# Seven small changes in one: decoding of picks on fewer columns, picks turned into one PSUM bank, low parts of U made by VectorE from the last query on, and reordered ends

## The chip, the cores and the metric

One core of a Trainium2 chip. The metric is the device time in microseconds (us) of one execution; lower is better. TensorE is PE in the rows (PEld is its weight load), VectorE DVE, ScalarE ACT, GpSimd POOL; SP is the queue that issues most transfers.

## What is computed

One encoder layer over 512 tokens of width 1024, in float32:

```
h = rms_norm(x);  P = h @ w_in                      # u_A, v_A, q, k, v
A = gelu(u_A) * (w_s . layer_norm(gelu(v_A)) + b)   # position mixing in chunks of 128
B = dilated windowed attention, 8 heads
x = x + concat(rms_norm(A), rms_norm(B)) @ w_out
xn = rms_norm(x)                                    # then PEER, per token:
  s1, i1 = top16(q1 . keys1);  s2, i2 = top16(q2 . keys2)        # per head, 128 keys each
  sc, ci = top16(s1[:, None] + s2[None, :])
  e = i1[ci // 16] * 128 + i2[ci % 16];  g = softmax(sc)
  x = x + sum over heads, picks of g * gelu(xn . U[e]) * V[e]     # 16384 experts
out = rms_norm(x)
```

## The kernel before

**Products in float32.** Both operands are split into a high part (ScalarE cast, `L80`, `L170`) and a low part (source minus high part: `L81`, `L181`); three products are accumulated.

**Stages, in order of time.** (1) Five projections in `proj` (`L252`), with norms, rotation (`rotate`) and head transposes between; at `L146` a root on ScalarE gives `xrs`, with which `rotate` reads the first projection's banks. The sums of squares under that root are made by `xsq` (`L151`). After the third projection `va` (`L373`) reads its banks through Gelu. (2) Attention (`L412` to `L447`) and the output projection. (3) Sixteen query products (`query`, `scores`), whose scores VectorE ranks (`top16`, `L618` to `L626`). (4) Routing: `decode` turns a pick's place in a list of 54 candidates into a row and a column, and looks both up by a one-hot of 16 by 16 per pick (`L681` to `L697`), for heads in groups of 3, 3 and 2 (`HG`); then `softmax`. VectorE does nearly all of it. (5) The banks: `turn` transposes a block's picks (`L824`), ScalarE copies them out (`L829`), and for every 8 tokens `hots` makes two one-hots on VectorE (`L855`, `L859`) whose 16 products (`L896`) give a dense matrix of gates, evacuated by ScalarE (`L876`) and stored to DRAM (`L884`). (6) The expert loop over 128 blocks e of 128 experts: acc of all three token blocks takes V's product (`vproduct`, `L1041`), while U's product (`product`, `L201`) runs 36 blocks ahead, and the gate is multiplied in (`L1026`). The fourth token block (128 tokens) is done by gathers of rows instead (`gather`, on GpSimd, VectorE). (7) Last sums, norm and output.

**What sets the order.** Each engine runs its queue in the order of the program. From stage 3's end to stage 6, products of U are strewn in by `ahead(n, limit)`: n matmuls of the running block (24 a block); a block's start also issues the load of the block two later and the high part of the block one later. Its low part is made by GpSimd in two halves inside `product` as long as `prog["pool"]` holds, and by VectorE in `los()` after that; `prog["pool"]` falls after `turn(0)`. `uraw`, `uhi` and `ulo` have two buffers each, so the load of block i+2 starts when high and low part of block i are made. The Gelu of a finished block (`flush`, `L768`) frees one of two PSUM banks `pu`.

**The end.** For the last two e the order is: (126, token blocks 0 and 1), (127, 0), (127, 1), (126, 2), (127, 2 in halves). Per block: sum and square (`final_sum`, `L1081`), gain (`L1092`), `root`, `finish` (`L1106`, `L1108`), store.

Of the kernel before, what the change touches and what calls it, by code (L numbers as in the profile page):

```python
# [20 lines left out]
NB = 4  # L21
# [19 lines left out]
UVB = 4  # L41
SLOW = 0.35
# [3 lines left out]
def peer_block(ctx: ExitStack, tc: tile.TileContext, A, out):  # L46
# [182 lines left out]
    warm(AF.Copy)  # L229
# [79 lines left out]
    def xsq(b):  # L309
        sq = tk.tile([128, 1024], F32, name="xs", bufs=4)  # L310
        sumsq(sq, xt[:, b, :], xss[:, b:b + 1])
# [60 lines left out]
    for b in range(NB):  # L372
        S.activation(va[:, b, :], ps[b], AF.Gelu_apprx_tanh, scale=xrs[:, b:b + 1], accum_out=lns[:, 0, b:b + 1])  # L373
# [274 lines left out]
    def decode(pool, lists, ci, outs):  # L648
# [3 lines left out]
        tl = lambda nm, dt: pool.tile(PK, dt, name=nm)  # L652

# [23 lines left out]
        wide = [128, n, TOPK, TOPK]  # L677
        ohs = []
        for r in (rw, cl):
            oh = pool.tile([128, nh, nb, TOPK, TOPK], BF16, name="oh", bufs=3 if pool is rt else 2)  # L680
            S.copy(oh.rearrange("p h b r c -> p (h b) r c"),  # L681
                   r.rearrange("p h b k -> p (h b) k")[:, :, :, None].to_broadcast(wide))
            ohs.append(oh)
        yield
        io = iota_b[:, None, None, 0:TOPK].to_broadcast(wide)
        o4 = [oh.rearrange("p h b r c -> p (h b) r c") for oh in ohs]
        for o in o4:
            V.tensor_tensor(o, o, io, op=ALU.is_equal)
        for p, o in enumerate(o4):
            V.tensor_tensor(o, o, fi.rearrange("p h b s k -> p (h b) s k")[:, :, p, None, :].to_broadcast(wide),  # L690
                            op=ALU.mult)
        yield
        for w in (8, 4, 2):
            for o in o4:
                V.tensor_tensor(o[:, :, :, 0:w], o[:, :, :, 0:w], o[:, :, :, w:2 * w], op=ALU.add)
        for oh, o in zip(ohs, outs):
            V.tensor_tensor(o, oh[:, :, :, :, 0], oh[:, :, :, :, 1], op=ALU.add)  # L697
# [15 lines left out]
    HG = (3, 3, 2)  # L713
    route = [rt.tile([128, DB, H, TOPK], F32, name=f"route{i}") for i in range(3)]
# [38 lines left out]
    def pick_head(h):  # L753
# [3 lines left out]
        for n in HG:  # L757
            if h == h0 + n - 1:
                steps.append(decode(rt, dense[1][:, h0:h0 + n], ci[:, h0:h0 + n], [r[:, h0:h0 + n] for r in by_head]))
# [42 lines left out]
    while steps:  # L802
        ahead(24, AHEAD)
        flush()
# [5 lines left out]
    for _ in range(4):  # L810
        ahead(36, AHEAD)
        flush()
# [5 lines left out]
    def turn(b):  # L818

        rows = []  # L820
        for nm, t, dt, scale in (("i2T", route[1], BF16, 1.0), ("i1T", route[0], BF16, 1.0),
                                 ("gT", route[2], F32, GSCALE)):
            ps = pr.tile([128, 512], F32, name="po" if nm == "i2T" else "tr")
            T.transpose(ps[:, :128], t[:, b].rearrange("p h k -> p (h k)"), ident)  # L824
            if nm == "i2T":

                idx = rt.tile([128, 16, 2, 8, 2], BF16, name="idxT", bufs=2)
            r = idx[:, :, len(rows), :, :] if dt is BF16 else rt.tile([128, 16, 8, 2], F32, name=nm)
            S.activation(r, ps[:, :128].rearrange("p (g t) -> p g t", t=8)[:, :, :, None].to_broadcast([128, 16, 8, 2]),  # L829
                         AF.Copy, scale=scale)  # L830
# [11 lines left out]
    prog["pool"] = False  # L842
# [4 lines left out]
    def hots(t8):  # L847
# [3 lines left out]
        idx, gw = tsc[b]  # L851
# [389 lines left out]
```

## Time and profile before

| | us |
|---|---|
| median of 3 runs (1487.87 to 1490.42) | 1488.34 |
| the profiled execution | 1490.96 |
| its span in the trace | 1489.2 |
| TensorE busy in it | 1453.4 (98%) |
| VectorE busy | 1159.6 (78%) |
| ScalarE busy | 641.3 (43%) |
| GpSimd busy | 283.6 (19%) |
| mean granted TensorE clock | 0.996 of full |

Busy TensorE is modelled: what its queue loses is seen in gaps between starts, and in stretches with a granted clock below 1. Where a row ends in [0.50 <-ACT ...], the engine sat idle 0.50 us before, and that released it.

### The profile page before, as it was taken

To read this page: it belongs to the slowest core of one execution; us is meant where nothing else is said; L and a number is where in the kernel's file an instruction comes from. 1 tells how busy PE (TensorE), PEld (TensorE's weight loads), DVE (VectorE), ACT (ScalarE), POOL (GpSimd) and SP (SyncE) were. 2 spreads that over 40 slices of the span, in tenths; PEclk is the share of its full clock that TensorE was granted. 3 is DMA by queue.
4 is the path that set the end of the run, shared out by engine and by line. 5 is a ranking of instruction groups with operands and counts; after the bars stand their busy time and mean duration, and the time that the engine had idled before them with its cause. 6 is when DMAs were issued, how large, how long until landed. Compare 5 with 4: busy or idle time off the path is not lost.

```text
span 1489.2 us, 21574 instructions
## 1 busy us (share of the span) xinstructions
PE 1453.4 (98%) x7945; PEld 1292.6 (87%) x7945; DVE 1159.6 (78%) x2415; ACT 641.3 (43%) x1088; POOL 283.6 (19%) x222
## 2 busy tenths in 40 slices
PE   8999999999899999999999999999999999999997
PEld 6878988888888899999999999999999999987785
DVE  4745554999899967779878787888787888877775
ACT  5455753344555544434333333333333333323334
POOL 0040002445500000012222222222222222211002
PEclk9999999999999999999999999999999999999999
DMA  6331032232366776469999999999999998988764
GB/s 217 106 99 57 22 114 104 86 91 96 110 230 256 261 291 214 135 228 378 355 351 329 315 338 321 327 334 336 347 326 333 331 328 308 348 286 299 250 212 160
DMA packets 128777, 358.52 MB, mean 241 GB/s; under 512 B 9120, under 2 KB 59808, under 8 KB 112288
## 3 DMA queue, kind: packets, MB, share of 16 engines
q1 hardware_dynamic: 103184, 197.75, 40.1%
q0 software_dynamic: 18432, 134.23, 23.6%
q10 hardware_dynamic: 7056, 25.18, 4.2%
q8 instruction: 62, 1.02, 0.3%
q14 instruction: 43, 0.35, 0.1%
HBM read 327.10 MB, written 30.02 MB: 240 GB/s over the span
## 4 chain that ended last, share of the span: by engine, by line
PE 78%; DVE 9%; DMA 5%; issue 3%; ACT 3%; POOL 1%; ACTq 0%; SPq 0%; DVEq 0%; POOLq 0%
PE pu L201 34%; PE acc L1041 30%; PE acc L252 6%; DMA vraw<-in_uv_dram 3%; DVE ohb L855 3%; DVE oha L859 2%; DVE ulo L181 1%; DMA uraw<-in_uT_dram 1%; PE tr L734 1%; PE pu L252 1%; PE tr L434 1%; POOL ulo L181 1%; PE acc L447 1%; DVE vlo L81 1%; DMA xt<-in_x_dram 1%
## 5 line engine op out<-in xcount | busy, mean ns | idle before, releaser
L201 PE MATMUL pu<-h2T,uhi 128*128 128x384 f32 (+2 forms) x2336 | 451.0, 342 | 3.2 <-ACT act L768 2.4
L201 PEld LDWEIGHTS pu<-h2T,uhi 128*128 128x128 f32 x2336 | 409.6, 189 | 19.4 <-ACT act L768 3.1
L987 POOL DMA_INDIRECT uv<-in_uv_dram,ei x128 | 170.6, 1333 | 830.1 <-DVE xlast L1002 318.0
L81 DVE TENSOR_TENSOR vlo<-vraw,vhi 128x1024 fp32r<-128x1024 f32 x128 | 156.8, 1225 | 154.9 <-ACT vhi L80 154.7
L80 ACT CAST vhi<-vraw 128x1024 fp32r<-128x1024 f32 x128 | 134.6, 1051 | 296.3 <-issue 188.6
L1041 PE MATMUL acc<-vhi,wahi 128*128 128x512 f32 x768 | 238.7, 391 | 1.9 <-ACT wahi L80 1.9
L1041 PE MATMUL acc<-vlo,wahi 128*128 128x512 f32 x768 | 238.2, 391 | 0.5
L1041 PE MATMUL acc<-vhi,walo 128*128 128x512 f32 x768 | 237.8, 391 | 0.0
L201 PE MATMUL pu<-h2T,ulo 128*128 128x384 f32 (+2 forms) x1168 | 234.1, 340 | 2.3 <-POOL ulo L181 2.3
L201 PEld LDWEIGHTS pu<-h2T,ulo 128*128 128x128 f32 x1168 | 203.7, 188 | 7.4 <-POOL ulo L181 2.9
L170 ACT CAST uhi<-uraw 128x1024 fp32r<-128x1024 f32 x144 | 150.7, 1047 | 61.1 <-DMA uraw<-in_uT_dram 47.6
L1041 PEld LDWEIGHTS acc<-vlo,wahi 128*128 128x128 f32 x768 | 143.8, 188 | 33.7 <-DVE vlo L81 2.4
L1041 PEld LDWEIGHTS acc<-vhi,walo 128*128 128x128 f32 x768 | 143.7, 188 | 31.5 <-DVE walo L81 0.9
L1002 DVE SCALAR_TENSOR_TENSOR xlast<-uv,dot,xlast 128x1024 f32<-128x1024 f32 x128 | 164.5, 1285 | 4.5
L1041 PEld LDWEIGHTS acc<-vhi,wahi 128*128 128x128 f32 x768 | 142.6, 188 | 26.9 <-ACT wahi L80 3.1
L768 ACT ACTIVATE act<-pu 128x384 f32<-128x384 f32 x128 | 62.9, 492 | 234.9 <-PE pu L201 234.5
L993 DVE SCALAR_TENSOR_TENSOR uv<-uv,h 128x1024 f32<-128x1024 f32 x128 | 153.7, 1219 | 6.7 <-DMA uv<-in_uv_dram,ei 6.7
L181 DVE TENSOR_TENSOR ulo<-uraw,uhi 128x1024 fp32r<-128x1024 f32 x116 | 141.5, 1220 | 22.1 <-ACT uhi L170 21.9
L181 POOL TENSOR_TENSOR ulo<-uraw,uhi 128x512 fp32r<-128x512 f32 x56 | 81.5, 1479 | 209.4 <-ACT uhi L170 203.7
L81 DVE TENSOR_TENSOR walo<-wa,wahi 128x384 fp32r<-128x384 f32 x128 | 70.7, 553 | 0.6 <-ACT wahi L80 0.6
L80 ACT CAST wahi<-wa 128x384 fp32r<-128x384 f32 x128 | 65.2, 509 | 13.0 <-DVE wa L1026 12.9
L1026 DVE TENSOR_TENSOR wa<-act,wt 128x384 f32<-128x384 f32 x128 | 70.5, 551 | 0.0
(258 smaller groups left out, 1475.4 us busy)
## 6 DMA issues: line engine op xcount, KB each, us to landing
uraw<-in_uT_dram SPq DMA_DIRECT2D x128, 512.0 KB, 5.9
vraw<-in_uv_dram SPq DMA_DIRECT2D x128, 512.0 KB, 5.3
wd<-wst ACTq DMA_DIRECT2D x48, 512.0 KB, 3.1
wt<-wd SPq DMA_DIRECT2D x32, 768.0 KB, 10.6
wraw<-in_w_in_dram SPq DMA_DIRECT2D x19, 512.0 KB, 3.6
uraw<-in_w_q_dram SPq DMA_DIRECT2D x16, 512.0 KB, 3.8
xT<-in_xT_dram SPq DMA_DIRECT2D x8, 256.0 KB, 3.9
xt<-in_x_dram SPq DMA_DIRECT2D x1, 2048.0 KB, 11.5
```

Of the source, the lines that this page charges most:

```text
L80: S.copy(hi, src)
L81: sub.tensor_tensor(lo, src, hi.bitcast(F32), op=ALU.subtract)
L170: S.copy(hi, raws[i])
L181: eng.tensor_tensor(lo[:, k, :], raws[i][:, k, :], hi[:, k, :].bitcast(F32), op=ALU.subtract)
L201: T.matmul(o, l[:, k, :], r[:, k, t0:n], start=(p == 0 and k == 0), stop=(p == 2 and k == KT - 1))
L252: T.matmul(out[b], l[:, b * 128:(b + 1) * 128], r[:, kk, :], start=(k == 0 and i == 0), stop=(k == KT - 1 and i == 2))
L768: S.activation(acts[e], o[:, :DT], AF.Gelu_apprx_tanh)
L987: G.indirect_dma_start(out=uvs[r].rearrange("p s d -> p (s d)"), out_offset=None, in_=A["uv"], in_offset=bass.IndirectOffsetOnAxis(ap=ei[: ...
L993: V.scalar_tensor_tensor(uv[:, 0, :], uv[:, 0, :], 1.0, h2, op0=ALU.mult, op1=ALU.mult, accum_out=d[:, 0:1])
L1002: V.scalar_tensor_tensor(xlast, uv[:, 1, :], d[:, 1:2], xlast, op0=ALU.mult, op1=ALU.add)
L1026: eng.tensor_tensor(wa.rearrange("p (c t) -> p c t", c=NWC), acts.pop(e).rearrange("p (c t) -> p c t", c=NWC), wts[e // WG][:, :, e % WG, ...
L1041: T.matmul(acc[b][n], l[:, c], r[:, n * 512:(n + 1) * 512], start=(e == 0 and i == 0), stop=(e == NK - 1 and i == 2))
```

## The change

It joins these edits (the line numbers of the new kernel are up to 60 higher):

1. Start: the first table that ScalarE loads holds Sqrt; two of the four sums of squares of `xsq` go to VectorE.
2. `warm(Gelu)` ahead of the last transposed head pair; `va` reads banks 1, 2, 3, then 0.
3. `decode`: the 16 sorted picks use only columns 0 to 7 for the picks 0 to 7 and all 16 for the rest, so the one-hot has 24 rows of 8 instead of 16 of 16; ScalarE's broadcast copies and VectorE's products are two each; the constant `iota_v` is made by GpSimd.
4. `prog["pool"] = False` already after the last query, with `los()` behind every `ahead`: VectorE makes the low parts of 11 blocks that GpSimd made.
5. `turn` writes three transposes into one bank; the gates' table has another layout.
6. `hots`: VectorE makes 7 of the 8 tokens' gate rows, ScalarE the eighth (`gated`, two small activations per 8 tokens).
7. One block of U is put ahead of the last stores (and one fewer after them).
8. The end: block 2's products of the last four e come last, half by half; blocks 0 and 1 are finished under them; the last two e's parts lie in the gather's buffers, and gathers are due one e earlier.

```diff
-    warm(AF.Copy)
+    warm(AF.Sqrt)
...
+        if b % 2:
+            V.scalar_tensor_tensor(sq, xt[:, b, :], 1.0, xt[:, b, :], op0=ALU.mult, op1=ALU.mult,
+                                   accum_out=xss[:, b:b + 1])
+        else:
+            sumsq(sq, xt[:, b, :], xss[:, b:b + 1])
...
+        if p == 3:
+            warm(AF.Gelu_apprx_tanh)
...
-    for b in range(NB):
+    for b in (1, 2, 3, 0):
         S.activation(va[:, b, :], ps[b], AF.Gelu_apprx_tanh, ...
...
+            oh = pool.tile([128, n, TOPK + K8, K8], BF16, name="oh", bufs=3 if pool is rt else 2)
+            S.copy(oh[:, :, 0:TOPK, :], flat.to_broadcast([128, n, TOPK, K8]))
+            S.copy(oh[:, :, TOPK:, :], flat[:, :, K8:, :].to_broadcast([128, n, K8, K8]))
...
+            V.tensor_tensor(o, o, iota_v[:, None, :, :].to_broadcast([128, n, TOPK + K8, K8]), op=ALU.is_equal)
+            V.tensor_tensor(o[:, :, TOPK:, :], o[:, :, TOPK:, :], f[:, :, :, K8:].to_broadcast(...), op=ALU.mult)
+            V.tensor_tensor(o[:, :, 0:TOPK, :], o[:, :, 0:TOPK, :], f[:, :, :, 0:K8].to_broadcast(...), op=ALU.mult)
...
+            V.tensor_tensor(o[:, :, K8:TOPK, :], o[:, :, K8:TOPK, :], o[:, :, TOPK:, :], op=ALU.add)
+        for w in (4, 2):
...
         else:
+            prog["pool"] = False
             ahead(12, AHEAD)
+            los()
...
     while steps:
         ahead(24, AHEAD)
+        los()
         flush()
         step()
...
+        ps = pr.tile([128, 512], F32, name=("tr", "po")[b % 2])
+        for j, t in enumerate((route[1], route[0], route[2])):
+            T.transpose(ps[:, j * 128:(j + 1) * 128], t[:, b].rearrange("p h k -> p (h k)"), ident)
...
-        wide = [128, 2, 8, NK // 2, 2]
+        wide = [128, 7, 2, NK // 2, 2]
...
+    def gated():
+        for a, c, gs, g in rest:
+            for s in range(2):
+                S.activation(a[:, 14 + s, :], c[:, 15, :], AF.Copy, scale=gs[:, g, s:s + 1])
+        rest.clear()
...
+    ahead(10 ** 6, AHEAD)
+    ahead(24, AHEAD + 5)
+    los()
     for j in range(per):
         store(j)
-    ahead(10 ** 6, AHEAD)
+    flush()
...
-    for _ in range(3):
+    for _ in range(2):
         ahead(24, AHEAD + 5)
...
+    lasts = range(NK - LASTV, NK)
+    for e in lasts:
+        vproduct(e, 2, (0,))
     for b in (0, 1):
+        sumsq(junk, xback[b], sums[b][:, 0, 0:1])
+        rs = inv_root(ex, sums[b][:, 0, 0:1], 1024)
+        for c in (slice(0, 512), slice(512, 1024)):
+            V.scalar_tensor_tensor(outs[b][:, c], xback[b][:, c], rs, fg[:, c], op0=ALU.mult, op1=ALU.mult)
+            Q.dma_start(out[b * 128:(b + 1) * 128, c], outs[b][:, c])
+        if b == 0:
+            final_sum(2, 0, 0, 512)
+    gain(2, 0, 512, V)
+    for e in lasts:
+        vproduct(e, 2, (1,))
...
+    V.tensor_scalar(xback[2][:, :512], outs[2][:, :512], rs, None, op0=ALU.mult)
+    S.activation(xback[2][:, 512:], outs[2][:, 512:], AF.Copy, scale=rs)
+    for q, c in ((Q, slice(0, 512)), (S, slice(512, 1024))):
+        q.dma_start(out[256:384, c], xback[2][:, c])
```

**The order on VectorE, second group of heads of the routing.** `cand` is the last list of candidates, `oh` the one-hot, `route` the looked-up keys. Before:

```order
L642 TENSOR_TENSOR cand<-s_2179 128x3x12
L642 TENSOR_TENSOR cand<-s_2179 128x3x8
L688 TENSOR_TENSOR oh<-oh,iota_b 128x2304 x2
L690 TENSOR_TENSOR oh<-oh,fi 128x2304 x2
L695 TENSOR_TENSOR oh<-oh 128x144x8 x2
L695 TENSOR_TENSOR oh<-oh 128x144x4 x2
L695 TENSOR_TENSOR oh<-oh 128x144x2 x2
L697 TENSOR_TENSOR route_2183<-oh 128x3x3x16
```

Now:

```order
L648 TENSOR_TENSOR cand<-s_2179 128x3x8
L182 TENSOR_TENSOR ulo<-uraw,uhi 128x1024 x2
L702 TENSOR_TENSOR oh<-oh,iota_v 128x1728 x2
L705 TENSOR_TENSOR oh<-oh,fi 128x9x64
L707 TENSOR_TENSOR oh<-oh,fi 128x9x128
L705 TENSOR_TENSOR oh<-oh,fi 128x9x64
L707 TENSOR_TENSOR oh<-oh,fi 128x9x128
L182 TENSOR_TENSOR ulo<-uraw,uhi 128x1024
L711 TENSOR_TENSOR oh<-oh 128x9x64 x2
L714 TENSOR_TENSOR oh<-oh 128x9x16x4 x2
L714 TENSOR_TENSOR oh<-oh 128x9x16x2 x2
L717 TENSOR_TENSOR route_2186<-oh 128x3x3x16
```

Low parts now stand between the steps of the decoding; one more stands ahead of the last query's ranking.

**The order on VectorE, third group of heads.** `fi` holds the picked lists, `gsum` the softmax's sums. Now (before, no `ulo` stood here):

```order
L688 CAST fi<-i_2180 128x192
L182 TENSOR_TENSOR ulo<-uraw,uhi 128x1024 x3
L728 TENSOR_REDUCE gsum<-route_2188 128x24
L729 RECIPROCAL gsum<-gsum 128x24
L730 TENSOR_TENSOR route_2188<-route_2188,gsum 128x8x3x16
L182 TENSOR_TENSOR ulo<-uraw,uhi 128x1024
L702 TENSOR_TENSOR oh<-oh,iota_v 128x1152 x2
L705 TENSOR_TENSOR oh<-oh,fi 128x6x64
L707 TENSOR_TENSOR oh<-oh,fi 128x6x128
```

Three low parts in a row, then a fourth; two more follow before the last additions.

**The order on ScalarE at the last stores.** `wst` is the evacuation of the last banks, `act` a Gelu. Before:

```order
L876 ACTIVATE wst<-acc 128x128x4 x2
L884 DMA wd<-wst 128x1024 x4
L170 CAST uhi<-uraw 128x1024
L768 ACTIVATE act<-pu 128x384
```

Now:

```order
L910 ACTIVATE wst<-acc 128x128x4 x2
L171 CAST uhi<-uraw 128x1024
L918 DMA wd<-wst 128x1024 x4
L789 ACTIVATE act<-pu 128x384
```

The cast that the next block waits for stands ahead of the four issues.

## Rows read from the trace of the kernel before

**Rows 1.** Stretches of the span: from:to in us, length, busy time of each engine (instructions), granted TensorE clock, DMA share, GB/s. A piece of the expert loop, then the banks.

```profile
900.00:1100.00 200.00, 200.00 (x1012) 182.07 (x1011) 165.93 (x235) 73.76 (x132) 47.06 (x35) 1.00 0.92 329
404.00:541.20 137.20, 131.29 (x1241) 121.11 (x1238) 134.56 (x118) 80.62 (x140) 0.00 (x0) 1.00 0.66 244
```

**Rows 2.** What TensorE waited for: us in total, times, longest.

```profile
PE acc L896 <- DVE oha L859: 3.9, 10, 0.7
PE pu L201 <- ACT act L768: 2.4, 1, 2.4
PE pu L201 <- POOL ulo L181: 2.3, 2, 2.0
PE tr L824 <- ACT idxT L829: 2.1, 3, 0.8
PE acc L252 <- ACT qraw L270: 2.1, 1, 2.1
PE po L824 <- DVE route L697: 1.5, 1, 1.5
PE acc L252 <- ACT va L373: 1.3, 1, 1.3
```

**Rows 3.** The start of the second projection: ScalarE's instructions in order of time (start, us, what, idle before); then, from the groups (us in total, mean ns | idle), VectorE's instruction of the kind that now makes a sum of squares.

```profile
28.43 1.05 ACT L151 ACTIVATE xs<-xt 128x1024 f32<-128x1024 f32 x1
29.59 1.28 ACT L146 ACT_TABLE_LOAD   x1
30.88 0.30 ACT L146 ACTIVATE xrs<-xss,eps 128x4 f32<-128x4 f32 x1
...
L1002 DVE SCALAR_TENSOR_TENSOR xlast<-uv,dot,xlast 128x1024 f32<-128x1024 f32 x128 | 164.5, 1285 | 4.5
```

**Rows 4.** A stretch as in Rows 1, right behind that wait.

```profile
32.30:35.60 3.30, 3.30 (x9) 2.60 (x10) 2.69 (x5) 2.54 (x4) 0.00 (x0) 0.60 0.00 0
```

**Rows 5.** VectorE in the routing, in order of time (xN: so many in the time given).

```profile
350.78 0.19 DVE L660 TENSOR_SCALAR mk<-cf 128x144 f16<-128x144 f16 x1
350.90 1.34 DVE L666 TENSOR_TENSOR at<-at,mk 128x144 f16<-128x144 f16 x1
...
365.06 2.63 DVE L688 TENSOR_TENSOR oh<-oh,iota_b 128x2304 bf16<-128x2304 bf16 x2
...
370.13 2.92 DVE L695 TENSOR_TENSOR oh<-oh 128x1152 bf16<-128x1152 bf16 x6
...
382.21 1.22 DVE L671 TENSOR_SCALAR rw<-ai 128x96 int32<-128x96 int32 x1
...
389.10 2.92 DVE L690 TENSOR_TENSOR oh<-oh,fi 128x1536 bf16<-128x1536 bf16 x2
391.94 5.32 DVE L695 TENSOR_TENSOR oh<-oh 128x768 bf16<-128x768 bf16 x6
397.18 0.56 DVE L697 TENSOR_TENSOR route<-oh 128x96 f32<-128x96 bf16 x2
```

**Rows 6.** GpSimd's low part at the time of the first slow instruction of Rows 5.

```profile
350.87 2.53 POOL L181 TENSOR_TENSOR ulo<-uraw,uhi 128x512 fp32r<-128x512 f32 x2 [2.19 <-ACT uhi L170]
```

**Rows 7.** VectorE in the banks: the first one-hot, then a low part and the starts after it.

```profile
401.17 1.22 DVE L855 TENSOR_TENSOR ohb<-iota_b,idxT 128x2048 bf16<-128x2048 bf16 x1
...
405.96 1.22 DVE L181 TENSOR_TENSOR ulo<-uraw,uhi 128x1024 fp32r<-128x1024 f32 x1
407.09 1.22 DVE L855 TENSOR_TENSOR ohb<-iota_b,idxT 128x2048 bf16<-128x2048 bf16 x1
408.35 1.22 DVE L859 TENSOR_TENSOR oha<-ohb,gw 128x2048 f16<-128x2048 bf16 x1
409.49 1.22 DVE L855 TENSOR_TENSOR ohb<-iota_b,idxT 128x2048 bf16<-128x2048 bf16 x1
```

**Rows 8.** From the tile of U's loads, stretch 345 to 404 us: time from issue to landing; and a cast of a high part on ScalarE there.

```profile
DMA to landing us min/median/max: 3.5/3.7/4.2
...
397.00 1.05 ACT L170 CAST uhi<-uraw 128x1024 fp32r<-128x1024 f32 x1 [5.05 <-DMA uraw<-in_uT_dram]
```

**Rows 9.** TensorE, in order of time: where it went on after the first transposed picks; of the 48 groups of bank products two that follow each other, and the last.

```profile
399.13 0.94 PE L201 MATMUL pu<-h2T,uhi 128*128 128x384 f32 x4
...
430.78 1.06 PE L896 MATMUL acc<-oha,ohb 128*128 128x128 f16 x16
...
433.49 1.07 PE L896 MATMUL acc<-oha,ohb 128*128 128x128 f16 x16
...
540.29 1.07 PE L896 MATMUL acc<-oha,ohb 128*128 128x128 f16 x16 [0.68 <-DVE oha L859]
```

**Rows 10.** ScalarE's smallest copy of the kind that `gated` adds; TensorE behind the last stores.

```profile
398.34 0.38 ACT L829 ACTIVATE idxT<-po 128x256 bf16<-128x256 f32 x1
...
546.11 3.04 PE L201 MATMUL pu<-h2T,uhi 128*128 128x384 f32 x16 [0.50 <-ACT uhi L170]
```

**Rows 11.** The end: TensorE's last piece in the chain that ended last (start and length in us, tile, line, instructions), then VectorE's first sum and last scaling of token block 2.

```profile
1413.43 62.23 PE acc L1041 x273
...
1480.58 0.69 DVE L1081 TENSOR_TENSOR fin<-acc,fin 128x512 f32<-128x512 f32 x1
...
1484.70 0.88 DVE L1108 TENSOR_SCALAR fin<-fin,sd 128x512 f32<-128x512 f32 x2
```

**Rows 12.** The page: U's loads, 512 KB each, median us from issue to landing over the whole kernel.

```profile
uraw<-in_uT_dram SPq DMA_DIRECT2D x128, 512.0 KB, 5.9
```

More of the change, by code (lines that the diff above doesn't have):

```diff
@@ L41 @@
 UVB = 4
+LASTV = 4
 SLOW = 0.35
@@ L364, in peer_block @@
     turning = heads_T("k", rot)
-    for _ in range(4):
+    for p in range(4):
+        if p == 3:
+            warm(AF.Gelu_apprx_tanh)
         next(turning)
         drain(gen, 2)
-    warm(AF.Gelu_apprx_tanh)
     drain(gen)
@@ L646, in candidates, with lookup_rows, decode @@
         return cand
-    def decode(pool, lists, ci, outs):
+    def lookup_rows(pool):
+        rows = pool.tile([128, 24, 8], BF16, name="iota_v")
+        for r0, r1, c0 in ((0, 16, 0), (16, 24, 8)):
+            G.tensor_copy(rows[:, r0:r1, :], iota[:, None, c0:c0 + 8].to_broadcast([128, r1 - r0, 8]))
+        return rows
+    def decode(pool, iota_v, lists, ci, outs):
         _, nh, nb, _ = PK = list(ci.shape)
@@ L867, in peer_block @@
     hot = [hots(0), hots(1)]
+    gated()
     ahead(24, AHEAD)
@@ L895, in peer_block @@
                     t = 4 * q + j
-                    T.matmul(pw[:, j, :], c[:, t, :], a[:, 8 * s + t, :], start=(s == 0), stop=(s == 1))
+                    T.matmul(pw[:, j, :], c[:, t, :], a[:, 2 * t + s, :], start=(s == 0), stop=(s == 1))
             t0 = (t8 % per) * 8 + 4 * q
@@ L946, in decoded @@
         def decoded(h):
-            return decode(gp, late[1][:, h:h + 4], gci[:, h:h + 4], [r[:, h:h + 4] for r in groute])
+            return decode(gp, iota_g, late[1][:, h:h + 4], gci[:, h:h + 4], [r[:, h:h + 4] for r in groute])
         for h in range(SOON, H):
@@ L1027, in wmul @@
                             acts.pop(e).rearrange("p (c t) -> p c t", c=NWC), wts[e // WG][:, :, e % WG, :], op=ALU.mult)
+    wlast = []
     def wsplit(e):
         if e in wmuls:
-            hi = ex.tile([128, DT], F32R, name="wahi")
-            lo = ex.tile([128, DT], F32R, name="walo")
+            if e < NK - 2:
+                hi = ex.tile([128, DT], F32R, name="wahi")
+                lo = ex.tile([128, DT], F32R, name="walo")
+            else:
+                if not wlast:
+                    wlast.append(ex.tile([128, 4, 512], F32R, name="wl", tag="uv", bufs=UVB))
+                hi, lo = (wlast[0][:, 2 * (e - NK + 2) + i, :DT] for i in range(2))
             split(hi, lo, wmuls.pop(e), V)
@@ L1164, in peer_block @@
             grs = root(gb, 2)
-        if e < NK - 2:
-            for b in range(DB):
+        if e < NK - 1:
+            for b in range(DB if e < NK - LASTV else DB - 1):
                 vproduct(e, b)
```

107 lines of the change are left out of this document (51 added, 56 removed).

## The prediction, made before the changed kernel ran

> **What bounds the kernel now.** I began with the page and with TensorE's share by stretches. The expert loop leaves nothing to gain: in 200 us of it TensorE is busy for 200.00 at full granted clock, with VectorE at 166 and ScalarE at 74 [rows 1]. The change adds or removes no matmul, so it can only win back time in which TensorE stands, and the list of TensorE's waits is the list of what is to be had [rows 2]: 2.1 us at the first root (`qraw`), 1.3 at the Gelus (`va`), 6.2 in the routing (Gelu 2.4, GpSimd's low parts 2.3, `route` 1.5), 2.1 at the turned picks, 3.9 at the gates' one-hots, and, outside the list, the end. In the banks VectorE is busy for 134.56 of 137.20 us and TensorE for 131.29 [rows 1]: there VectorE is the bound. Most of the seven edits can be priced; the doubtful one is the low parts, since in the routing VectorE is already the engine that others wait for.
>
> **The first root.** ScalarE makes four sums of squares (1.05 us each), loads a table (1.28) and takes the root at 30.88 [rows 3]. Two sums go to VectorE, at 1.29 us each by its nearest instruction [rows 3], and the load goes to the start. ScalarE's part is then over some 2.9 us earlier, but the root waits for VectorE's second sum, which stands behind a low part whose cast comes one sum (1.05) earlier; I put the root at about 29.2, 1.7 earlier, and TensorE's 2.1 us [rows 2] shrink to 0.4. [...] Gain **3.0** (1.7 if the clock falls all the same, 3.6 if the wait goes fully). [...]
>
> **The Gelus.** The table load moves ahead of the last head pair's casts, where ScalarE waits in any case, and the first bank that is waited for is read first instead of second. Of the 1.3 us [rows 2] I take **1.0**; no less than 0.5 (the casts come later by part of the load), no more than 1.4.
>
> **The routing.** VectorE's queue in it is one chain, with the end of `route` at 397.18 + 0.56 = 397.74 [rows 5]. By parts:
> - Less decoding. One-hot and product shrink by a quarter (24 x 8 of 16 x 16), the first addition by half. Of the second group of heads, 2.63 for the one-hots [rows 5], the same for the products, 2.92 for the additions, that is 1.9 us; of the third, two thirds as large, 1.2; of the first, which lies ahead, 1.9 with what GpSimd cost it. Together 5.0 earlier.
> - Less contention. While GpSimd makes a low part from 350.87 on [rows 6], an instruction like one that took 0.19 us takes 1.34; six are slowed so, from the one at 350.90 to the one at 382.21 [rows 5], by some 1.05 us each: 6.3. The third group's products take 2.92 where two thirds of 2.63 are 1.8, and its additions 5.32 where two thirds of 2.92 are 2.0 [rows 5]: 1.1 and 3.3. Together 10.7 earlier, as GpSimd makes no low part there any more.
> - Low parts. Eleven, each 1.14 us from start to start [rows 7]: 12.5 later.
> - New waits. A load takes 3.7 us to land and the cast 1.05 [rows 8], and a load may start only when the low part two blocks back is made. Blocks 6, 7 and 8 now stand in one row on VectorE: 8 begins 4.7 after the end of 6, of which 7 fills 1.14, so VectorE stands 3.6. Block 9's cast stands on ScalarE behind a table load (1.28), a Gelu and the third group's copies, some 2.4 more; block 11 repeats the first case with much of it filled, 0.8. Together 6.8, in place of the 1.8 that VectorE waited for copies of one-hots: 5.0 later.
>
> Sum: -5.0 - 10.7 + 12.5 + 5.0 = +1.8, so `route` is ready at about 399.6. TensorE cannot run ahead into this: block 1's low part stands on VectorE behind three rankings, so TensorE waits some 6 us early, and about 2 at the transposes, in place of its old 6.2. It goes on at about 400.1 instead of 399.13 [rows 9]: 1.0 lost. ScalarE turns the three transposes out of one bank in a row, the gates' table gets two tiny instructions more, and the first one-hot begins at about 402.6 instead of 401.17 [rows 7], since the old start, too, was set by the chain behind `route`. Lost on VectorE **1.4**, with bounds from a gain of 3 (no new waits: 5.0 less, and then TensorE's own work is what remains) to a loss of 8 (loads landing in 5.9, the kernel's median [rows 12]: each wait on a load 2.2 longer, and the casts behind them).
>
> **The banks.** VectorE ran from 401.17 to the last group at 540.29 [rows 7, 9]: 139.1 us. One step of it is 1.26 + 1.14 [rows 7]; the gates' part loses an eighth, 0.145, 48 times: 7.0. The table of each block costs two tiny instructions, 0.5 in all: 132.6. From 402.6 that ends at 535.2. TensorE's own floor is a step of 433.49 - 430.78 = 2.71 us [rows 9], 47 times 127.4 after a first group at about 405.0 (one one-hot and one gate table behind 402.6): 532.4. VectorE still sets it, narrowly; the pauses at the transposes (2.1) [rows 2] vanish under it. Last group 535.3 instead of 540.29: gain **5.0** for routing and banks together, between -3 and +8. ScalarE gets 96 activations of 128 columns. The nearest row is 256 columns at 0.38 [rows 10]; half of that and the whole of it are the bounds, 18 to 36 us on top of its 80.62 [rows 1], so 99 to 117 of some 133: cover enough, if its queue does not stand badly. [...]
>
> **The last stores.** The cast that waited behind four issues now stands first: the 0.50 us of [rows 10] go. Gain **0.5**; below nothing only if the gates' load came late, and the next user of it comes five blocks later.
>
> **The end.** TensorE's last 273 matmuls take 62.23 us, 0.228 each; VectorE's first sum of block 2 starts at 1480.58 and its last scaling ends at 1485.58 [rows 11]. Now 24 matmuls of block 2 stand last, so sums, root and output of blocks 0 and 1 run under 24 x 0.228 = 5.5 us of them. Counted through by the durations there, VectorE and ScalarE need some 11.8 us from block 1's last matmul instead of 9.7 from one 2.7 later, so the last store starts 0.6 sooner, and from two queues, with blocks 0 and 1 stored already: **1.0** (0 to 2.5). In the last 150 us TensorE's few waits for V's loads stay as they are: 0, within 1.5 either way.
>
> **Sum.** 3.0 + 1.0 + 5.0 + 0.5 + 1.0 = 10.5 us off the profiled span of 1489.2, that is 1478.7. The profiled execution took 1490.96 and lies 2.6 above the median of the runs, 1488.34; off that median it makes **1477.8**.
>
> **Rivals.**
> - *The queue waits less than I count* (VectorE's low parts find their casts ready, since loads land while it ranks). For it: ScalarE's copies of one-hots are shorter. Against: two buffers. Up to 3 more, then TensorE's floor in the banks holds: 1474.5. Chance 0.17.
> - *The queue waits longer*: loads of 5 to 6 us. Six more us at `route`: about 1483. For it, the kernel's median of 5.9 [rows 12]; against, 3.5 to 4.2 in that stretch [rows 8]. Chance 0.13.
> - *ScalarE becomes the bound of the banks*: its two small activations wait for VectorE's one-hot, and evacuations, casts and store issues queue behind them. The banks' gain of 5 goes: about 1483. For it, 56% busy turned to 75 to 88%; against, one-hots are made two steps ahead of need. Chance 0.09.
> - *Slower than before*: low parts in VectorE's queue make the ring of two U buffers serial (low part, load, cast, low part), with the one-hot steps between. Each us of landing puts off `route` by some 2.8 us, as three waits on loads and two casts hang in the chain; from a landing of 7.3 us on, the whole 10.5 is eaten, from 8.2 on it is slower by more than 0.2%. At 8.5 it makes 1491.5. No row there is above 4.2. Chance 0.05.
> - *The edits at the start do nothing for the clock*: inside the forecast's range.
>
> **How the numbers follow.** Forecast 0.56, at 1477.8, its own range 1474.8 to 1480.8. A measurement here tells 0.2% (3 us) from no change. Faster by that: all of the forecast and of the first rival, most (0.17) of the second and third: 0.90. Within it 0.06, from the tails of those and of the fourth. Slower 0.04. The range of 1471.5 to 1484.5 takes in forecast and first three rivals, with the unpriced ends of the last stretch.
>
> **What would show it.** Right: TensorE's wait for `qraw` under 0.6 us with the granted clock at 1.00 behind it; no wait for GpSimd; one long wait, about 6 us, of U's product for a VectorE low part near 352; `route` between 398 and 401; bank groups 2.7 to 2.8 us apart, the last starting near 535; the last matmul some 9.5 us earlier. Wrong: `route` ready later than 404; VectorE's one-hots of 1728 columns taking more than 1.1 us each; ScalarE named as what the bank products wait for.

## The result

| | before | changed |
|---|---|---|
| median, us | 1489.0 (6 runs) | 1480.17 (6 runs, 1477.83 to 1482.53) |
| ratio to before, 95% interval | | 0.9942 [0.9928, 0.9956] |
| the profiled execution / its span | 1490.96 / 1489.2 | 1482.49 / 1480.7 |
| TensorE busy; VectorE; ScalarE; GpSimd | 1453.4; 1159.6; 641.3; 283.6 | 1449.8; 1153.4; 657.6; 244.0 |

8.8 us faster by the medians, 8.5 by the two spans; forecast were 10.5, and 1480.17 lies inside the range. The numbers leave out three single executions that took 3600 to 3900 us, one of the kernel with edit 7 undone and two of the kernel before.

**The profile after.** The list of what TensorE waited for (us in total, times, longest), which answers to [rows 2]:

```profile
PE pu L202 <- DVE ulo L182: 7.6, 2, 7.1
PE acc L253 <- DVE wph L106: 4.8, 1, 4.8
PE acc L930 <- DVE oha L883: 2.4, 5, 0.7
PE tr L847 <- DVE route L717: 1.9, 1, 1.9
PE pu L202 <- ACT uhi L171: 1.2, 1, 1.2
PE acc L1092 <- ACT wl L81: 1.0, 1, 1.0
...
PE pu L202 <- ACT act L789: 0.7, 1, 0.7
```

`qraw`, `va`, GpSimd's low parts and the turned picks are gone from it. New are one long wait for a low part by VectorE, 1.2 for a high part and 1.0 for the last high part of the gated activations. The 4.8 for `wph` isn't new: it is TensorE's wait for its first weights, at the very start, and the kernel before has the same 4.8.

Where the time was won and given back is read from the same instruction in both kernels. Three moments of the kernel before that its rows above don't have (TensorE by time: start, us, what): the last query's scores, the first product of V, the last matmul.

```profile
346.11 1.05 PE L734 MATMUL tr<-keys,qT 128*128 128x128 f32 x8
...
567.02 0.63 PE L1041 MATMUL acc<-vhi,wahi 128*128 128x512 f32 x2
...
1478.21 0.39 PE L1041 MATMUL acc<-vhi,walo 128*128 128x512 f32 x1
```

The changed kernel, TensorE: these, and the long wait, the transposes, the first and last bank group and the 1.2 us wait.

```profile
341.40 1.05 PE L755 MATMUL tr<-keys,qT 128*128 128x128 f32 x8
...
344.38 2.94 PE L202 MATMUL pu<-h2T,uhi 128*128 128x384 f32 x16
354.44 2.93 PE L202 MATMUL pu<-h2T,ulo 128*128 128x384 f32 x8 [7.11 <-DVE ulo L182]
...
396.73 0.52 PE L847 MATMUL tr<-ident,route 128*128 128x128 f32 x3 [1.86 <-DVE route L717]
...
401.62 1.05 PE L930 MATMUL acc<-oha,ohb 128*128 128x128 f16 x16 [0.20 <-DVE oha L883]
...
533.19 1.07 PE L930 MATMUL acc<-oha,ohb 128*128 128x128 f16 x16 [0.21 <-DVE oha L883]
...
556.36 3.06 PE L202 MATMUL pu<-h2T,uhi 128*128 128x384 f32 x16 [1.22 <-ACT uhi L171]
...
560.64 0.63 PE L1092 MATMUL acc<-vhi,wahi 128*128 128x512 f32 x2
...
1469.92 1.52 PE L1092 MATMUL acc<-vl,wl 128*128 128x512 f32 x6
```

And VectorE: its low parts in the routing (what ended the idle time before them in brackets), the last look-up, the first one-hot of the banks.

```profile
353.18 1.21 DVE L182 TENSOR_TENSOR ulo<-uraw,uhi 128x1024 fp32r<-128x1024 f32 x1
...
358.31 2.35 DVE L182 TENSOR_TENSOR ulo<-uraw,uhi 128x1024 fp32r<-128x1024 f32 x2
...
365.33 1.23 DVE L182 TENSOR_TENSOR ulo<-uraw,uhi 128x1024 fp32r<-128x1024 f32 x1 [0.65 <-ACT uhi L171]
...
382.35 1.23 DVE L182 TENSOR_TENSOR ulo<-uraw,uhi 128x1024 fp32r<-128x1024 f32 x1 [3.46 <-ACT uhi L171]
...
387.38 1.23 DVE L182 TENSOR_TENSOR ulo<-uraw,uhi 128x1024 fp32r<-128x1024 f32 x1 [2.42 <-ACT uhi L171]
...
393.34 1.23 DVE L182 TENSOR_TENSOR ulo<-uraw,uhi 128x1024 fp32r<-128x1024 f32 x1 [0.79 <-ACT uhi L171]
...
396.03 0.56 DVE L717 TENSOR_TENSOR route<-oh 128x96 f32<-128x96 bf16 x2
...
399.22 1.22 DVE L879 TENSOR_TENSOR ohb<-iota_b,idxT 128x2048 bf16<-128x2048 bf16 x1
400.47 1.09 DVE L883 TENSOR_TENSOR oha<-ohb,gw 128x1792 f16<-128x1792 bf16 x1
401.48 1.22 DVE L879 TENSOR_TENSOR ohb<-iota_b,idxT 128x2048 bf16<-128x2048 bf16 x1
```

| up to | before | changed | lead | won in this part | forecast |
|---|---|---|---|---|---|
| last query's scores | 346.11 | 341.40 | 4.7 | 4.7 | 4.0 |
| VectorE's first one-hot of the banks | 401.17 [rows 7] | 399.22 | 1.95 | -2.8 | -1.4 |
| last bank group | 540.29 [rows 9] | 533.19 | 7.1 | 5.15 | 6.4 |
| first product of V | 567.02 | 560.64 | 6.4 | -0.7 | 0.5 |
| end of the last matmul | 1478.60 | 1471.44 | 7.2 | 0.8 | 0 |
| end of the span | 1489.2 | 1480.7 | 8.5 | 1.3 | 1.0 |

Three parts missed the forecast downward, by 3.9 us together, and three upward, by 1.8. That the sum is only 2 us off is partly luck.

### The profile page after: what moved, and what is told of

Its sections match the earlier page's. It is cut to its first block, busy times and chain, and to the rows that moved or that the text cites. A ratio compares the mean times of both kernels' runs of the same rounds, so it can differ in the third digit from the quotient of the medians.

```text
span 1480.7 us, 21686 instructions
## 1 busy us (share of the span) xinstructions
PE 1449.8 (98%) x7945; PEld 1291.6 (87%) x7945; DVE 1153.4 (78%) x2445; ACT 657.6 (44%) x1186; POOL 244.0 (16%) x200
## 4 chain that ended last, share of the span: by engine, by line
PE 75%; DVE 13%; DMA 6%; ACT 4%; issue 2%; ACTq 0%; SPq 0%; DVEq 0%
PE acc L1092 30%; PE pu L202 29%; PE acc L253 8%; DMA vraw<-in_uv_dram 4%; DVE ohb L879 3%; DVE ulo L182 2%; DVE oha L883 2%; DMA uraw<-in_uT_dram 1%; PE pu L253 1%; PE tr L440 1%; PE acc L453 1%; DVE vlo L82 1%; PE po L453 1%; ACT uhi L171 1%; ACT vhi L81 1%
## 5 line engine op out<-in xcount | busy, mean ns | idle before, releaser
L1092 PE MATMUL acc<-vhi,wahi 128*128 128x512 f32 x756 | 235.0, 391 | 0.4 <-ACT wahi L81 0.4
L1092 PE MATMUL acc<-vlo,wahi 128*128 128x512 f32 x756 | 234.4, 391 | 0.2
L1092 PE MATMUL acc<-vhi,walo 128*128 128x512 f32 x756 | 234.2, 391 | 0.0
L182 DVE TENSOR_TENSOR ulo<-uraw,uhi 128x1024 fp32r<-128x1024 f32 x127 | 154.8, 1220 | 27.8 <-ACT uhi L171 27.7
L182 POOL TENSOR_TENSOR ulo<-uraw,uhi 128x512 fp32r<-128x512 f32 x34 | 44.2, 1324 | 178.6 <-PE acc L253 104.6
## 6 DMA issues: line engine op xcount, KB each, us to landing
xt<-in_x_dram SPq DMA_DIRECT2D x1, 2048.0 KB, 10.7
```

Source lines behind the costliest of these rows:

```text
L182: eng.tensor_tensor(lo[:, k, :], raws[i][:, k, :], hi[:, k, :].bitcast(F32), op=ALU.subtract)
L1092: T.matmul(acc[b][n], l[:, c], r[:, n * 512:(n + 1) * 512], start=(e == 0 and i == 0), stop=(e == NK - 1 and i == 2))
```

## The experiments

Each is an edit of the changed kernel, timed beside the kernel before; its own 1480.17 (0.9942) is what they are held against. Edits 5 and 8 were not undone by themselves; for them the trace alone speaks. (The title counts seven changes; the list has eight, and the numbers here are the list's.) A and B are the theories in the expectation above each result. One ratio is known to about 0.0014, so that two of them differ for certain only by 0.002, some 3 us.

**Edits 1 and 2 undone.**

```diff
-    warm(AF.Sqrt)
+    warm(AF.Copy)
...                                  # all four sums by sumsq(), warm(Gelu) behind the head pairs
-    for b in (1, 2, 3, 0):
+    for b in range(NB):
```

> The changed kernel with edits 1 and 2 undone (first table without the root, four sums of squares on ScalarE, Gelu's table loaded behind the last head pair, banks read 0 to 3). Theory A (what TensorE wins at the start it keeps to the end): the wait of 2.1 us with 3.3 us at a granted clock of 0.60 behind it and the wait of 1.3 us come back, the last query scores start 4.6 us later, all that follows too: 1484.8, ratio to before 0.997. Rival B (the VectorE chain of ranking and routing takes the start's gain back): the last looked-up key comes less than 2 us later, time 1480 to 1482, ratio 0.994 to 0.995.

1483.15 us, 0.9962 [0.9949, 0.9975]. TensorE waits again, 1.7 us for `qraw` and 1.3 for `va`; the last scores start 4.1 us later (345.48), the transposes only 2.9 (399.58). Between A and B: the wins are there where they were forecast, but whether a part is taken back by VectorE's chain behind them can't be told. The twelve executions spread over 10 us (1479.35 to 1489.47). And in the profiled one VectorE came first in the race told of below (its additions took 0.81), while in the changed kernel's GpSimd did (2.96): that alone can hide a part of the 4.1. Behind the 1.7 us wait TensorE's granted clock was 1.00 at once:

```profile
32.60:36.00 3.40, 3.37 (x14) 2.75 (x15) 2.78 (x5) 2.65 (x4) 0.00 (x0) 1.00 0.00 0
```

(a stretch as in [rows 4], where it was 0.60 behind a wait of 2.06).

**Edit 3 undone** (the code of before in `decode`, from the one-hots on).

```diff
-            oh = pool.tile([128, n, TOPK + K8, K8], BF16, name="oh", ...)
+            oh = pool.tile([128, nh, nb, TOPK, TOPK], BF16, name="oh", ...)
...
-        for w in (4, 2):
+        for w in (8, 4, 2):
```

> The changed kernel with edit 3 undone: one-hots of 16 by 16 per pick and three halving additions. Theory A (the routing of the changed kernel is one VectorE chain, in which the smaller decoding saves 1.9, 1.9 and 1.2 us for its three groups): the last key is looked up 4 to 5 us later than in the changed kernel (transposes at 396.7 there), time 1484 to 1485, ratio to before 0.997. Rival B (VectorE has waits for casts in the routing, 7.3 us in all, which longer decoding would only fill): the last key 1 to 2 us later, time 1481 to 1482, ratio 0.995.

1484.32 us, 0.9970 [0.9957, 0.9983], 4.15 us slower than the changed kernel; the transposes start at 399.89, 3.2 later, the first bank group 4.1 later. A, by the time; the 3.2 at the transposes are less than the 4 to 5 that it gave. VectorE still waits 6.7 us for casts there, so the longer decoding did not fill these waits.

**Edit 4 undone.**

```diff
-            prog["pool"] = False
             ahead(12, AHEAD)
-            los()
...                                  # no los() behind the two ahead() of the routing either
     drain(turn(0))
+    prog["pool"] = False
```

> The changed kernel with edit 4 undone: GpSimd makes the 11 low parts of U again until the first transposed picks. Theory A (the sum of the prediction: what VectorE wins by the end of the contention, about 10, is less than the 12.5 for eleven low parts and the 7.3 that its trace shows of waits for casts): VectorE's chain to the last looked-up key becomes 8 to 10 us shorter than in the changed kernel (end 396.6 there, 387 to 389 here), TensorE's 7.1 us wait for a low part goes, some 2 us of waits for GpSimd come; about 1474, ratio to before 0.990. Rival B (the contention is worth more than the low parts and the waits, so edit 4 is itself a gain): the last key at 397 or later, 1481 to 1485, ratio 0.995 to 0.998.

1475.04 us, 0.9912 [0.9900, 0.9925]: 5.1 us faster than the changed kernel. A: the time is within 1 us of the 1474 that it gave, the long wait is gone, and TensorE waits 2.8 for GpSimd. The last key is looked up at 389.56, 7.0 earlier, where A gave 8 to 10. In both profiles GpSimd came first at 328 us, so the race plays no part in the comparison. The contention is back (VectorE, then GpSimd, with four half low parts in 10.84 us that take 5.05 a few us earlier):

```profile
369.66 1.28 DVE L670 CAST cf<-ci 128x96 f16<-128x96 uint32 x1
...
385.79 3.30 DVE L714 TENSOR_TENSOR oh<-oh 128x384 bf16<-128x384 bf16 x4
...
388.99 0.57 DVE L717 TENSOR_TENSOR route<-oh 128x96 f32<-128x96 bf16 x2
```

```profile
353.82 5.05 POOL L182 TENSOR_TENSOR ulo<-uraw,uhi 128x512 fp32r<-128x512 f32 x4 [4.77 <-ACT uhi L171]
361.27 10.84 POOL L182 TENSOR_TENSOR ulo<-uraw,uhi 128x512 fp32r<-128x512 f32 x4 [2.41 <-ACT uhi L171]
```

So one of the joined edits takes back a part of what the others win: by the medians the eight together are worth 8.8 us, the other seven 13.7.

**The gates part of edit 6 undone.**

```diff
-        wide = [128, 7, 2, NK // 2, 2]
+        wide = [128, 8, 2, NK // 2, 2]
...
-        rest.append((a, c, gs, g))
```

> The changed kernel with the gates part of edit 6 undone: VectorE makes all 8 tokens' gate rows, ScalarE's 96 small activations are gone. Theory A (VectorE's queue is the bound of the banks): 48 x 0.145 = 7.0 us more VectorE work between the first one-hot and the last group, of which TensorE's pauses take up little: banks 139 to 141 us long where the changed kernel has 134.0, time 1485 to 1487, ratio to before 0.998. Rival B (the banks got shorter by the transposes in one bank, and ScalarE or TensorE's own floor of 2.71 us a step bounds them now): banks 134 to 136, time 1480 to 1482, ratio 0.994 to 0.995.

1485.48 us, 0.9978 [0.9969, 0.9987]. VectorE needs 139.7 us from the first one-hot (397.91) to the last group (537.64). A: VectorE is the bound of the banks, and the eighth token is worth 5.3 us. The same stretch of the banks from each kernel, this one first, then the changed one (busy time of TensorE, its loads, VectorE, ScalarE, GpSimd):

```profile
401.60:533.20 131.60, 125.92 (x1179) 115.97 (x1178) 129.93 (x118) 77.59 (x136) 0.00 (x0) 1.00 0.67 244
```

```profile
401.60:533.20 131.60, 129.06 (x1227) 120.47 (x1227) 129.22 (x122) 104.26 (x234) 0.00 (x0) 1.00 0.66 247
```

VectorE is as busy; TensorE has got 3.1 us more done, and ScalarE, at 104 of 131.6, is still covered.

**Edit 7 undone.**

```diff
+    for j in range(per):
+        store(j)
     ahead(10 ** 6, AHEAD)
-    ahead(24, AHEAD + 5)
-    los()
-    for j in range(per):
-        store(j)
```

> The changed kernel with edit 7 undone: the last stores' four issues stand ahead of the cast of the block of U again. Theory A (the wait of 1.22 us that TensorE has in the blocks of U before the loop comes from a load of U that is queued behind the gates' and V's loads, in either order; the edit itself wins its 0.5): from the last bank group to the first product of V 27.5 to 28.5 us (27.45 in the changed kernel, 26.73 before), time 1480 to 1481. Rival B (the block put ahead shifts the loads into each other, so the edit loses 0.7): 26.5 to 27.0 us, time 1479.4, both ratios 0.994.

1479.74 us, 0.9949 [0.9935, 0.9963]; 27.15 us from the last group to the first product of V. Neither A nor B: TensorE waits 0.9 for the cast behind the stores (0.5 in the kernel before), and the later wait is gone in this profile. Edit 7 is worth nothing that can be measured.

**Room for more loads.**

```diff
+            u = i - NQ
+            if 2 <= u < 12 and u % 2:
+                raws[i] = rt.tile([128, KT, 128], F32, name="urawb", tag="ohb", bufs=3)
+            else:
                 raws[i] = upool.tile([128, KT, 128], F32, name="uraw")
```

> The changed kernel with room for more loads in the routing: every second block of U from the fourth to the twelfth is loaded into one of three buffers that lie idle until the banks, so that a load no longer waits for the low part two blocks back. Nothing else is changed. Theory A (VectorE's 7.3 us of waits for casts in the routing come from the ring of two load buffers): these waits fall under 2.5, the last key is looked up some 3 us earlier, and then TensorE's own work behind its 7.1 us wait is the bound, since it had only 3.1 us of waits left there: 1477, ratio to before 0.992. Rival B (the casts come late by ScalarE's queue, its table loads, Gelus and one-hot copies, or by the two buffers of high parts): the waits stay above 5, time within 1 us of the changed kernel's 1480.2, ratio 0.994.

1480.40 us, 0.9940 [0.9926, 0.9955]: no gain. In the routing there is one: the transposes start at 394.45, 2.3 earlier. VectorE's waits for casts and buffers fall from 7.9 only to 5.8 (stretch 338 to 405):

```profile
DVE ulo L186 <- ACT uhi L175: 4.3, 4, 2.2
...
DVE ulo L186 <- PE pu L206: 1.5, 1, 1.5
```

What is left isn't the loads. The 2.2 are a cast behind a table load, a Gelu and one-hot copies on ScalarE; in the 1.5 a low part waits until TensorE is through with the one that its own buffer holds; the other casts stand behind a table load or a Gelu. B explains what is left, A what went. And the 2.3 us are given back before the expert loop (TensorE by time):

```profile
551.32 1.55 PE L206 MATMUL pu<-h2T,ulo 128*128 128x384 f32 x8
555.09 4.62 PE L206 MATMUL pu<-h2T,uhi 128*128 128x384 f32 x16 [2.22 <-ACT uhi L175]
```

```profile
555.09:559.70 4.61, 4.61 (x17) 4.61 (x18) 3.93 (x5) 2.85 (x5) 0.00 (x0) 0.63 0.17 51
```

The load behind that cast stands in SP's queue after the gates' load, which waits for the last stores, and two loads of V. TensorE waits 2.2 us and then runs 16 matmuls in 4.62 instead of 2.93, at a granted clock of 0.63: 3.9 us lost.

**The same, and GpSimd for two more low parts.**

```diff
-            prog["pool"] = False
             ahead(12, AHEAD)
-            los()
...
         ahead(24, AHEAD)
+        turns += 1
+        if turns == 1:
+            prog["pool"] = False
         los()
```

> As the kernel with room for more loads, and besides GpSimd makes the low parts of the second and third block of U, which fall into VectorE's ranking; VectorE makes those from the fourth block on. Theory A (TensorE's 7.1 us wait and the ring of load buffers together are what the routing loses): TensorE's wait for a low part falls under 2, the last key comes at about 389 to 391 instead of 396.6, time 1473 to 1474, ratio to before 0.990. Rival B (VectorE's chain is as long as before since GpSimd's two low parts slow the decoding of the first group, and the casts stay late): the last key at 394 or later, time 1477 to 1480, ratio 0.992 to 0.994.

1479.15 us, 0.9941 [0.9928, 0.9954]. B: the transposes start at 395.00. The two low parts slow the decoding, the second group's by the trace, by about what VectorE saves (a cast that took 0.24 in the changed kernel, at 346.02, takes 1.21), and TensorE's wait is cut into 4.1 and 1.8, for VectorE's next two low parts.

**The race.** The kernel with edit 7 undone has the code of the changed one up to the end of the banks, and still its transposes start 2.5 us earlier (394.22). The two profiles part at 328 us, where VectorE ends the first group's decoding while GpSimd makes a low part. The changed kernel, both engines by time (xN: so many in the time given):

```profile
328.40 1.29 POOL L182 TENSOR_TENSOR ulo<-uraw,uhi 128x512 fp32r<-128x512 f32 x1 [3.29 <-ACT uhi L171]
...
328.50 1.50 DVE L711 TENSOR_TENSOR oh<-oh 128x576 bf16<-128x576 bf16 x1
```

The kernel with edit 7 undone:

```profile
328.38 0.81 DVE L711 TENSOR_TENSOR oh<-oh 128x576 bf16<-128x576 bf16 x2
...
328.75 4.14 POOL L182 TENSOR_TENSOR ulo<-uraw,uhi 128x512 fp32r<-128x512 f32 x1 [3.75 <-ACT uhi L171]
```

Whoever starts first, here by 0.1 or 0.4 us, runs on. Where GpSimd does, the first addition takes 1.50, and both together 2.96; where VectorE does, both take 0.81, and GpSimd's half low part 4.14 instead of 1.29. It ends at 332.89, 1.29 after 331.6, when VectorE ends not these two additions but all of its two-input instructions behind them that stand without a gap. Where GpSimd is first, VectorE's first addition ends 0.31 us behind GpSimd's half (330.00 and 329.69); where VectorE is, GpSimd is held up for longer than one of VectorE's instructions.

Being first at the additions doesn't settle it. In the kernel with the end's steps moved (below) VectorE was first too, at 0.82, and met GpSimd right behind, in its list of candidates, which takes 0.60 in the changed kernel; its transposes start at 396.34, as late as the changed kernel's:

```profile
331.31 2.85 DVE L648 TENSOR_TENSOR cand<-s 128x48 f32<-128x48 f32 x5
```

Two experiments move VectorE's additions out of the race, ahead of the ranking, or behind the list of candidates.

```diff
+            if c == 12:
+                step()                # the first group's additions
             scores(c - 1)
-            if c < NQ:
+            if c < NQ and c != 12:
                 step()
```

> The changed kernel with one step moved on VectorE: the additions that end the first group's decoding stand ahead of the ranking of the twelfth scores instead of behind it, some 3.5 us earlier, when GpSimd makes no low part. Theory A (the executions of the changed kernel differ by 2 to 3 us because at 328.4 us GpSimd's low part and VectorE's additions start within 0.4 us of each other: whoever comes second is held up by some 2.2 us, and VectorE's place at the end of the routing moves by as much): the additions never meet a low part, all executions lie near the lower ones of the changed kernel, median 1478, spread under 2 us (4.7 in the changed kernel), ratio to before 0.993. Rival B (the differences between executions come from the loads of U before the expert loop, 4 to 8.5 us to landing): median 1480, spread as before.

1477.71 us, 0.9929 [0.9915, 0.9944], five executions from 1476.91 to 1479.98. The additions take 0.82 at 324.35, the list of candidates 0.60, and the transposes start at 393.18, 3.5 earlier. That is A, by the trace: the contention at this place is gone. By the time it isn't shown, since the two ratios differ by 0.0013; and a spread of 3.1 in five executions, more than A allowed, can't be told from 4.7 in six.

> The changed kernel with the same additions put 0.6 us later instead, behind the list of candidates that follows them, so that GpSimd's low part always comes first. Theory A (the race for one of the two engines to run first): the additions always wait for GpSimd, median 1481 to 1482, ratio to before 0.995 to 0.996, none of the executions below 1479. Rival B: median 1480, executions down to 1478.

1480.20 us, 0.9939 [0.9923, 0.9955], from 1478.27 to 1482.28. A's price was too high: the list of candidates meets GpSimd's first half (from 328.95) and takes 1.71 instead of 0.60; the additions begin at 330.21, between GpSimd's two halves, run at full speed and hold up the second (the two halves take 5.27 instead of 2.54). So VectorE waits for one half and not for two: it gets in between two instructions of GpSimd's, as GpSimd did not between VectorE's. That all of the spread comes from this place isn't shown.

**The end.**

```diff
-            grs = root(gb, 2)
+        if e == NK - 2:
+            grs = root(gb, 2)
...
-        if b == 0:
-            final_sum(2, 0, 0, 512)
+    final_sum(2, 0, 0, 512)
     gain(2, 0, 512, V)
```

> The changed kernel with two steps of its end moved: the root of the gathered token block stands behind the splits of the last e instead of ahead of them, and block 2's first sum stands behind the output of blocks 0 and 1 instead of between them. Theory A (ScalarE's table load ahead of the last cast makes TensorE wait 1.0 us, and after the last matmul VectorE stands behind block 1's output, which waits for a root that ScalarE makes behind a square of block 2): the wait of 1.0 goes, and from the last matmul's end to the end of the span 7.1 us pass instead of 9.3; 3 us less in all: 1477, ratio to before 0.992. Rival B (ScalarE's and VectorE's work at the end is as long in any order): the end stays at 9 us or more, gain 1 us at most, 1479.2.

1478.07 us, 0.9925 [0.9912, 0.9938]; by the time not to be told from the changed kernel. In the trace the 1.0 us wait for `wl` is gone, and 8.2 us pass from the last matmul's end to the end of the span, against 9.3: half of what A gave it, since VectorE, which has no pause any more, comes to block 2's last sums only 1.4 us behind the last matmul.

**Three at once**: edit 4 undone, this end, and one U block's load ahead of the first loads for the expert loop.

```diff
-    for _ in range(2):
+    for _ in range(3):
         ahead(24, AHEAD + 5)
...
     vload(0)
     vload(1)
-    for _ in range(2):
+    for _ in range(1):
         ahead(24, AHEAD + 5)
```

> Three things at once: the low parts by GpSimd until the first transposed picks (1475.0 in its run), the two moved steps of the end, and the first loads of the gates and V put one block of U later, so that a load of U stands ahead of them in the queue. Theory A (each acts in its own place): 1475.0 less 1.0 and 2.2 at the end, less 1.5 for waits on loads of U before the loop: 1470.3, ratio to before 0.988; from the last bank group to the first product of V 26 to 27 us. Rival B (gates and V now come late themselves, so TensorE waits for the first product of V instead): 28 us or more there, 1472 to 1473.

1470.25 us, 0.9879 [0.9864, 0.9893]. A by the time, and partly by luck: the end gave 1.1 of the 2.2 that A counted, and the start was 1.5 us earlier in this execution than in the one of edit 4 undone. The loads hold: from the last bank group to the first product of V it takes 26.2 us (28.1 with edit 4 undone), with no wait in the six blocks of U:

```profile
525.30 1.07 PE L927 MATMUL acc<-oha,ohb 128*128 128x128 f16 x16 [0.23 <-DVE oha L880]
...
551.49 0.72 PE L1089 MATMUL acc<-vhi,wahi 128*128 128x512 f32 x2
```

**And the moved additions, with block 2's sums ahead of its gains.**

```diff
+        if b == 0:
+            V.tensor_tensor(xback[2][:, :512], acc[2][0], xback[2][:, :512], op=ALU.add)
+    sumsq(junk[:, :512], xback[2][:, :512], ss[:, 0, 0:1])
...
+    gain(2, 0, 512, V)               # behind the last sums; the other gain behind the root's sums
```

> The fastest kernel so far (1470.25: low parts by GpSimd, the steps of the end moved, U's load ahead of the gates' first load) with the additions of the first group moved ahead as in the first of these runs, and at the end VectorE's sums of block 2 ahead of its gains. Theory A (in that kernel the additions met no low part in its profile; the end is VectorE's throughput): 0.5 us less at the end and an equal routing, 1469.5, ratio to before 0.987. Rival B (the moved additions now meet another low part, since all of TensorE's queue stands earlier): 1471 to 1473.

1469.91 us, 0.9870 [0.9853, 0.9886], the fastest; not to be told from the one before. 10.3 us below the changed kernel. The end takes 7.5 us instead of 8.2; the last key comes no earlier (388.50 and 387.63).

## Why the prediction held, and where it was off

- **The first root: 3.0 forecast, 3.3 measured.** The root starts at 28.44 instead of 30.88 [rows 3], TensorE doesn't wait (in one kernel with the same start, the one with the additions put later, it waits 1.1 for `qraw`), and from 30 to 36 us its granted clock is 1.00 (0.60 in [rows 4]). The 3.3 are the lead of the second projection's matmuls behind that place (35.60 and 32.31): 2.06 of wait and some 1.3 of clock. The clock's part belongs to that execution of the kernel before, since with edits 1 and 2 undone a wait of 1.7 left it at 1.00, and the same matmuls came 2.5 later and not 3.3. In the forecast's 3.0 the clock stands with 1.3, the author's estimate from the 3.3 us at 0.60 in [rows 4] (3.3 x 0.4); no other run here shows that loss, and in the changed kernel the clock is 1.00. **The Gelus: 1.0, measured 1.3**, the whole wait.
- **The routing: loss of 1.4 forecast, 2.8 measured.** The step that priced the new waits held almost to the number: 3.6, 2.4 and 0.8 for blocks 8, 9 and 11 against 3.46, 2.42 and 0.79, and TensorE's long wait was 7.1 instead of 6, some 5 us earlier than the 352 named (4.7 of them the start's lead). A wait of 0.65 at block 4 was missed. Another part failed in "the first, which lies ahead, 1.9 with what GpSimd cost it": the first group's decoding won 1.3 (VectorE reaches its one-hots 4.4 us earlier than before, its look-up 5.6), as in this execution GpSimd came first at 328 and its additions took 2.96 instead of 0.81. The two make some 1.1 of the 1.4. Where VectorE came first, with edit 7 undone, the routing cost nothing or little: its lead was 4.35 at the last scores and 4.45 at the banks' first one-hot (396.72). The moments named as "what would show it" (`route` 398 to 401, the last group near 535) left the start's 4.0 us out; with them they would have read 394 to 397 and 531, and the trace has 396.59 and 533.19.
- **The low parts themselves.** The sum had the answer that it didn't draw: 10.7 won from the contention against 12.5 + 5.0 for low parts and waits says that edit 4 is a loss. Alone it costs 5.1 us of the time.
- **The banks: 6.4 forecast, 5.15 measured.** VectorE's gate rows take 1.01 from start to start (400.47 to 401.48 above) instead of 1.14, so the eighth is worth 0.13 and not 0.145 a step (0.7 of the difference); the rest is not settled. ScalarE's 96 small activations take 399 ns each, just over the upper bound that was drawn from a 256-column row, and 0.30 from the first one's start to the next one's where two stand in a row. ScalarE stayed covered all the same.
- **The last stores: gain of 0.5 forecast, loss of 0.7 measured.** The 0.5 wait went, and 1.22 came five blocks on. SP's queue there, and the cast that waits:

```profile
544.96 0.38 SPq L1050 DMA_DIRECT2D wt<-wd  x1
545.39 1.22 SPq L1052 DMA_DIRECT2D vraw<-in_uv_dram  x2
546.71 3.19 SPq L164 DMA_DIRECT2D uraw<-in_uT_dram  x2
```

```profile
555.26 1.04 ACT L171 CAST uhi<-uraw 128x1024 fp32r<-128x1024 f32 x1 [3.76 <-DMA uraw<-in_uT_dram]
```

  The load issued at 546.71 lands 8.5 us later, behind 768 KB of gates and two loads of V. In the kernel before the same load landed after 7.5 us, also behind them, and its cast still ended 0.8 us ahead of TensorE:

```profile
561.03 1.05 ACT L170 CAST uhi<-uraw 128x1024 fp32r<-128x1024 f32 x1 [1.64 <-DMA uraw<-in_uT_dram]
562.86 2.93 PE L201 MATMUL pu<-h2T,uhi 128*128 128x384 f32 x16
```

  "Below nothing only if the gates' load came late" looked at the gates and not at what is queued behind them. The order of the loads is the cause: seven kernels here with edit 7 and the old order of the loads have this wait (1.0 to 2.2), and the one with three edits at once, which has one more load of U ahead of them, has none.
- **The tail and the end: 1.0 forecast, 0.8 + 1.3 measured.** TensorE waits 1.4 us in the tail instead of 1.9, though its last wait, 1.0, is for a cast behind a table load.
- **Rivals.** Neither end of the queue's waits (none, or all long) came true, ScalarE didn't become the bound, and loads landed in 3.5 to 4.7 us in the routing, far from the 8 of the slow rival.

## What to carry to other kernels

Work moved from a slower engine to the one that others wait for must be set against both prices at once, the contention it ends and the waits it brings into that queue; here they came out 5 us against it, and only because the edits were joined did the sum still win. Look at where two engines that hold each other up start within half a microsecond: moving one of them by a few us cost nothing here and brought a later stage 3.5 us forward in the one profile (2.5 in the medians, less than these runs can tell apart). And a load that is needed soon belongs ahead of larger ones in its queue: here its buffer was free 0.7 us before it was issued, and what it lost it lost in landing behind them (8.5 us).

## What the runs showed of the hardware

Contention goes both ways, and is dear for the second comer: GpSimd's two half low parts take 2.54 us alone and 5.39 where VectorE came first; VectorE's two additions 0.81 alone and 2.96 where GpSimd did. One half of GpSimd's took 4.14 and ended 1.29 after VectorE's run of two-input instructions, while VectorE got in between GpSimd's two (330.21). VectorE's ranking wasn't slowed: in the changed kernel three MAX8 over 128 scores took 0.66 to 0.68 beside GpSimd and without. TensorE's granted clock stayed at 1.00 behind a wait of 1.7 us. It was 0.63 in the stretch behind one of 2.2, where 16 matmuls took 4.62 us instead of 2.93; and 0.50 right behind the 7.1 us wait, where 8 matmuls took 2.93 instead of 1.55. A table load on ScalarE (1.28 us) that waited for nothing began 0.00 to 0.03 us after the instruction before it, and the activation behind it followed 0.01 to 0.02 us later, in the kernel before (12 loads) and in the changed one (11).
